# Modulation vectors on ScalarE and GpSimd, a scan for the summed decays, shorter Newton steps

## The chip, the core and the metric

The kernel runs on one core of a Trainium2 chip. The metric is the device time of one execution in microseconds (us), lower is better. TensorE is written PE here, VectorE DVE, ScalarE ACT, GpSimd POOL and SyncE SP, as the profile names them; PEld is PE's weight load.

## What is computed

Two transformer blocks run one after the other on 512 tokens of width 1024, in float32. What matters here is the first layer of the first block:

```python
mod = c_act @ ada_w[l] + ada_b[l]
sh1, sc1, g1, sh2, sc2, g2 = jnp.split(mod, 6, axis=-1)
hn = modulate(rms_norm(h, norm_mix_g[l]), sh1, sc1)
mix = hgrn2_mixer(hn, ...)       # chunks of 16 tokens, state carried along
h = h + g1 * mix
h = h + g2 * peer_ffn(modulate(rms_norm(h, norm_ffn_g[l]), sh2, sc2), ...)
```

and inside the mixer, for chunks of 16 tokens, `cum = jnp.cumsum(lfc, axis=2)`, the sum of the log decays within the chunk. Each `rms_norm` is `xf * lax.rsqrt(jnp.mean(xf * xf) + 1e-6)`. There are 14 modulation vectors of 1024 (six for each of two layers, two for the shared keys and values), each the product of one row of 1024 with a 1024 x 1024 matrix that is read once.

## The kernel before, in words

The 512 tokens are four tiles of 128. The first stage (0 to about 290 us) computes most of the 14 modulation vectors and, beside them, the mixer for tiles 0 and 1. Then the expert lookup `peer` (4 tiles, twice) gathers 64 rows of 8 KB for each token; beside it run the mixer for tiles 2 and 3, the attention of the second layer and the start of the second block. The last stage (from about 2250 us) is the mixture of experts of the second block.

`ada_vec` (line 243) makes one modulation vector, in two halves of 512 columns. Each half is a tile `aw` of 128 x 8 x 512 (2 MB), loaded in one transfer; four such buffers turn in a ring. Vectors 0 and 1 are loaded on SP's queue, the later ones on POOL's queue, where nothing else stands in this stage. A half is reduced over its 8 slices in one of two ways. With `pe` set, PE multiplies by the 128 x 32 tile `ca32` into PSUM (`ad<-aw,ca`, line 113; the program has 8 multiplications of 32 x 512 for a half, the trace shows 16), and ACT copies the sum to `aacc` (line 270). Without it DVE does one multiplication (line 272) and seven multiply-adds (line 275). Then PE adds `aacc` over the 128 rows, to columns (`ad<-kf,aacc`) or to a row (`ad<-aacc,kf`). The list `ADA` (line 1720) says which vector goes which way: 3, 12 and 7 on PE, five others on DVE. Vectors 8 and 9 (`ADA_MID`) and 10 and 11 (`ADA_LATE`) are on PE too.

`hgrn` (line 346) is the mixer, a sequence of steps that `Beside` interleaves with the vectors: normed rows are turned into `hTa` (`norm_T`, line 181), then there are eight heads; for each head PE makes the projections `pj`, ACT makes exponentials, tanh and logarithms, and DVE makes the products. Lines 414 to 420 are the sum of the log decays in chunks of 16: four rounds, each with one DVE addition (line 417) and one ACT copy of the part that has no partner (line 419), in turn between `lfa` and `lfb`.

`rsqrt` (line 161) is a Newton iteration on DVE for one or two columns: three operations to start (lines 164 to 166), then three rounds of three (lines 168 to 170). It is called in every norm.

Within an engine instructions run in the order in which a scheduler put them when the kernel was built; by that order an instruction that waits holds all that stand behind it on its engine. The rings of buffers decide when a transfer can start.

Of the kernel before, what the change touches and what calls it, by code (L numbers as in the profile page):

```python
# [11 lines left out]
F32 = mybir.dt.float32  # L12
I32 = mybir.dt.int32
U32 = mybir.dt.uint32
AF = mybir.ActivationFunctionType
ALU = mybir.AluOpType
# [4 lines left out]
P = 128  # L21
# [4 lines left out]
EPS = 1e-6  # L26
# [64 lines left out]
class K:  # L91
# [69 lines left out]
    def rsqrt(self, x, n, scale):  # L161
        nc = self.nc
        m, t, r = (self.sp.tile([P, n], F32, tag=f"{w}{n}", name=f"{w}{n}") for w in ("rsm", "rst", "rsr"))
        nc.vector.tensor_scalar(m, x, scale, EPS, op0=ALU.mult, op1=ALU.add)
        nc.vector.tensor_scalar(t.bitcast(I32), m.bitcast(I32), 1, None, op0=ALU.logical_shift_right)
        nc.vector.tensor_scalar(r.bitcast(I32), t.bitcast(I32), -1.0, float(0x5F3759DF), op0=ALU.mult, op1=ALU.add)
        for _ in range(3):
            nc.vector.tensor_tensor(out=t, in0=m, in1=r, op=ALU.mult)
            nc.vector.scalar_tensor_tensor(t, t, -0.5, r, op0=ALU.mult, op1=ALU.mult)
            nc.vector.scalar_tensor_tensor(r, t, 1.5, r, op0=ALU.add, op1=ALU.mult)  # L170
        return r

# [67 lines left out]

    def ada_vec(self, j, col, pe, tag="ad"):
        nc = self.nc
        pool = self.ap
        if col:
            pc = self.psum(tag)
            dst = self.cp.tile([P, 8], F32, name=f"ac{j}")
        else:
            dst = self.dp.tile([1, D], F32, name=f"ar{j}")  # L250
        for half in range(2):
            ch = 2 * j + half
            src = self.a["adaw"][ch]
            if self.aring:
                w = self.aring.tile([P, 8, 512], F32, tag="aw", name="aw")
                (nc.sync if j < 2 else nc.gpsimd).dma_start(w, src)
                w = [w[:, k, :] for k in range(8)]
            else:
                w = []
                for k in (0, 4):  # L260
                    g = self.gp.tile([P, 2 * D], F32, tag="g", name="g").rearrange("p (k n) -> p k n", k=4)
                    nc.sync.dma_start(g, src[:, k : k + 4, :])
                    w += [g[:, i, :] for i in range(4)]
            acc = pool.tile([P, 512], F32, tag="aacc", name="aacc", bufs=2)
            if pe:
                ps = self.psum(tag)
                for k in range(8):
                    g = 32 * (k % 4)
                    self.mm(ps[g : g + 32, :], self.ca32[:, k, :], w[k], start=k < 4, stop=k >= 4, tile_position=(0, g))
                nc.scalar.copy(acc, ps)  # L270
            else:
                nc.vector.tensor_scalar(acc, w[0], self.ca[:, 0:1], None, op0=ALU.mult)
                for k in range(1, 8):
                    nx = pool.tile([P, 512], F32, tag="aacc", name="aacc", bufs=2)
                    nc.vector.scalar_tensor_tensor(nx, w[k], self.ca[:, k : k + 1], acc, op0=ALU.mult, op1=ALU.add)
                    acc = nx
            if col:
                for q in range(4):
                    i = 4 * half + q
                    self.mm(pc[:, i : i + 1], acc[:, q * P : (q + 1) * P], self.ones[:, 0:1])  # L280
            else:
                rw = pool.tile([1, 512], F32, tag="arw", name="arw", bufs=3)
                nc.sync.dma_start(rw, self.a["adab"][ch : ch + 1, :])
                pr = self.psum(tag)
                self.mm(pr[0:1, :], self.ones[:, 0:1], acc)
                nc.vector.tensor_tensor(out=rw, in0=rw, in1=pr[0:1, :], op=ALU.add)
                nc.scalar.dma_start(dst[:, half * 512 : half * 512 + 512], rw)
        if col:
            n = 76 + 8 * COL.index(j)
            nc.vector.tensor_tensor(out=dst, in0=pc[:, 0:8], in1=self.cv[:, n : n + 8], op=ALU.add)  # L290
            self.col[j] = dst
        else:
            self.row[j] = dst
# [52 lines left out]
    def hgrn(self, tiles, gs, sh, bufs, whole=False):  # L346
        nc = self.nc
        es = ExitStack()
        nt = len(tiles)
        T = nt * P  # L350
        pa = self.pool("hgA", es=es)

        def ew(shape, tag, b=bufs):
            return pa.tile([P] + shape, F32, tag=tag, name=tag, bufs=b)

        def zeroed(name):
            z = pa.tile([P, T], F32, name=name)
            nc.vector.memset(z, 0.0)
            return z

        scb = [zeroed(f"scb{j}") for j in range(2)]
        kx = {n: zeroed(f"kx{n}") for n in (16, 32, 64)}
        qx = {n: zeroed(f"qx{n}") for n in (32, 64)}
        half = lambda x, n, j: x.rearrange("p (c j t) -> p c j t", j=2, t=n)[:, :, j, :]
        ch = lambda x, n: x.rearrange("p (c t) -> p c t", t=n)
        hTa = pa.tile([P, KC, T], F32, name="hTa")
# [6 lines left out]
        for hd in range(8):  # L373
            q2 = hd % 2
            if q2 == 0:
                w = self.weights(self.a["hgw"][4 * (hd // 2) + 3])
# [7 lines left out]
            w = self.weights(self.a["hgw"][4 * (hd // 2) + q2])  # L384
# [25 lines left out]
            lf = ew([T], "lfa")  # L410
            nc.scalar.activation(lf, e, AF.Ln, scale=self.lb[:, hc], bias=1.0)
            nc.scalar.activation(e, e, AF.Ln, bias=1.0)
            nc.vector.tensor_tensor(out=lf, in0=lf, in1=e, op=ALU.subtract)
            cum = lf
            for n, d in enumerate((1, 2, 4, 8)):
                nx = ew([T], "lfb", 1) if n % 2 == 0 else ew([T], "lfa")
                nc.vector.tensor_tensor(out=ch(nx, 16)[:, :, d:], in0=ch(cum, 16)[:, :, d:],
                                        in1=ch(cum, 16)[:, :, : 16 - d], op=ALU.add)
                nc.scalar.copy(ch(nx, 16)[:, :, :d], ch(cum, 16)[:, :, :d])
                cum = nx  # L420
            yield

            qs = ew([T], "qs")
# [7 lines left out]
            for n in (16, 32, 64):  # L431
                x = half(kx[n], n, 0)
                nc.vector.tensor_tensor(out=x, in0=half(cum, n, 0)[:, :, n - 1 : n].broadcast_to([P, T // (2 * n), n]),
                                        in1=half(cum, n, 0), op=ALU.subtract)
# [4 lines left out]
                else:  # L439
# [5 lines left out]
                                        in1=half(cum, n, 0)[:, :, n - 1 : n].broadcast_to([P, T // (2 * n), n]), op=ALU.add)  # L445
# [3 lines left out]
                                    in1=ch(cum, P), op=ALU.subtract)  # L449
# [36 lines left out]
            for i in range(nt):  # L486
                sl = slice(i * P, (i + 1) * P)
                nc.scalar.activation(o2[:, sl], po[:, sl], AF.Square, accum_out=ss[:, i : i + 1])
            r = self.rsqrt(ss, nt, 0.25 / P)
            on = ew([T], "ks")  # L490
            nc.vector.tensor_tensor(
                out=ch(on, P), in0=ch(po[:, :T], P), in1=r.unsqueeze(2).broadcast_to([P, nt, P]), op=ALU.mult)
# [19 lines left out]
        if whole:  # L512
            w = [self.weights(self.a["hgwo"][c]) for c in range(4)]
# [4 lines left out]
        else:  # L518
            for c in range(4):
                w = self.weights(self.a["hgwo"][c])  # L520
# [1067 lines left out]
    def run(self):  # L1588
# [23 lines left out]
        bg.advance(5 / 36)  # L1612
        for n, (j, pe) in enumerate(ADA):
            if n == 3:
# [102 lines left out]
        self.es.close()  # L1717


ADA = ((3, 1), (4, 0), (2, 0), (12, 1), (13, 0), (6, 0), (7, 1), (5, 0))  # L1720
ADA_LATE = ((10, 1), (11, 1))
COL = (0, 1, 6, 7, 12, 13)
ADA_MID = ((8, 1), (9, 1))
# [97 lines left out]
```

## Time and profile before

| | |
|---|---|
| median of 3 runs | 2770.45 us (2767.01 to 2771.69) |
| the profiled execution | 2769.54 us |
| its span, first to last instruction | 2767.7 us |
| TensorE's mean granted clock | 0.930 |
| PE, PEld busy | 85%, 54% of the span |
| DVE, ACT, POOL busy | 69%, 29%, 28% |
| HBM traffic over the span | 355 GB/s |

The span is 1.84 us shorter than the execution that it was recorded in. The profile has the busy time of each engine, a list of instruction groups by line with what they waited for, a timeline, and a chain of waits: the work that ended last, followed back from the last instruction, at each step to what released it.

### The profile page before, as it was taken

What the parts mean: (1) busy time and instruction counts of PE and PEld (TensorE: products, weight loads), DVE (VectorE), ACT (ScalarE), POOL (GpSimd) and SP (SyncE); (2) the same over time, 40 slices, a digit from 0 to 9 for tenths busy, and PEclk for the clock granted to TensorE, in tenths of its full rate; (3) what the DMA queues carried; (4) which work ended last, traced back from release to release, by engine and by line L of the source; (5) the groups of instructions that cost most, each with busy time, mean ns of one, the idle gap of its engine ahead of it and who ended that gap; (6) DMA issues with size and microseconds to landing.
All of it is one profiled execution on the core that took longest, in us unless ns stands there. A gap on an engine that the chain in (4) does not pass through costs nothing.

```text
span 2767.7 us, 30061 instructions
## 1 busy us (share of the span) xinstructions
PE 2340.0 (85%) x9714; PEld 1481.2 (54%) x9714; DVE 1918.3 (69%) x5370; ACT 795.0 (29%) x1891; POOL 777.0 (28%) x607
## 2 busy tenths in 40 slices
PE   5999888877988888579988858779999999988886
PEld 3786556644556555146656525437688754433322
DVE  3876898998996689984578799978787551111114
ACT  2543245562222632121383112142311310000001
POOL 0000123334333344443344334544440001111110
PEclk9999999998999889789999869889999999999999
DMA  9875889999989899999989889987999868999996
GB/s 413 325 281 189 321 311 357 380 378 375 374 356 406 330 350 384 336 369 401 370 307 371 326 312 341 363 327 289 390 413 363 298 237 364 424 426 425 423 425 280
DMA packets 124607, 976.22 MB, mean 353 GB/s; under 512 B 16830, under 2 KB 18238, under 8 KB 23584
## 3 DMA queue, kind: packets, MB, share of 16 engines
q0 software_dynamic: 82384, 591.04, 54.8%
q1 hardware_dynamic: 39280, 375.51, 33.4%
q10 hardware_dynamic: 2784, 7.73, 0.8%
q8 instruction: 79, 1.29, 0.2%
q14 instruction: 80, 0.66, 0.1%
HBM read 963.84 MB, written 19.43 MB: 355 GB/s over the span
## 4 chain that ended last, share of the span: by engine, by line
PE 43%; DVE 28%; DMA 16%; issue 6%; ACT 6%; POOL 1%; ACTq 0%; SPq 0%; POOLq 0%; DVEq 0%
PE pj L113 16%; DVE g L697 8%; DMA we<-in_we_dram 7%; DMA g<-in_uv_dram,ex 7%; PE acc L113 6%; PE gu L113 6%; PE mm L113 4%; DVE acc L716 4%; PE rt L113 3%; PE y L113 3%; DVE y L947 3%; PE ad L113 2%; POOL g L694 1%; DMA w<-in_hgw_dram 1%; PE mm L123 1%
## 5 line engine op out<-in xcount | busy, mean ns | idle before, releaser
L694 POOL DMA_INDIRECT g<-in_uv_dram,ex x512 | 695.3, 1358 | 1157.9 <-DVE acc L716 439.6
L113 PE MATMUL acc<-g,dg 128*128 128x512 f32 x1056 | 588.3, 690 | 191.4 <-ACT dg L708 191.0
L697 DVE SCALAR_TENSOR_TENSOR g<-g,hn 128x1024 f32<-128x1024 f32 x512 | 621.7, 1218 | 102.2 <-DMA g<-in_uv_dram,ex 100.0
L113 PEld LDWEIGHTS acc<-g,dg 128*128 128x128 f32 x1056 | 213.4, 215 | 440.2 <-ACT dg L708 261.3
L716 DVE SCALAR_TENSOR_TENSOR acc<-g,wt,acc 128x1024 f32<-128x1024 f32 x240 | 306.9, 1279 | 3.5
L113 PE MATMUL gu<-we,xT 128*64 128x512 f32 x1120 | 258.9, 601 | 19.3 <-DMA we<-in_we_dram 18.5
L113 PE MATMUL pj<-hT,w 128*128 128x256 f32 (+1 forms) x1136 | 216.2, 345 | 4.6 <-DMA w<-in_win_dram 3.1
L113 PEld LDWEIGHTS pj<-hT,w 128*128 128x128 f32 x1136 | 186.0, 193 | 39.6 <-issue 16.8
L113 PEld LDWEIGHTS gu<-we,xT 128*64 128x64 f32 x1120 | 100.5, 138 | 166.3 <-issue 115.2
L113 PE MATMUL pj<-hTa,w 128*128 128x256 f32 x768 | 181.1, 381 | 0.9 <-DVE sg L408 0.9
L113 PE MATMUL pj<-w,hT 128*128 128x256 f32 (+1 forms) x832 | 179.1, 373 | 0.0
L1433 DVE SCALAR_TENSOR_TENSOR th<-th,gu 128x256 f32<-128x256 f32 x35 | 14.7, 421 | 233.3 <-ACT th L1432 233.3
L701 ACT ACTIVATE wt<-hid 128x2 f32<-128x2 f32 x256 | 51.8, 203 | 422.8 <-DVE g L697 421.5
L113 PEld LDWEIGHTS pj<-w,hT 128*128 128x128 f32 x832 | 153.7, 192 | 27.4 <-issue 8.4
L1398 POOL DMA_INDIRECT xg<-xd,gi x31 | 32.0, 1033 | 449.3 <-PE tr L123 233.1
L113 PEld LDWEIGHTS pj<-hTa,w 128*128 128x128 f32 x768 | 141.2, 191 | 24.2 <-issue 5.6
L113 PE MATMUL y<-we,hT 128*64 128x512 f32 x560 | 143.3, 597 | 3.4 <-ACT hT L1442 0.4
L113 PE MATMUL rt<-hn2T,w 128*128 128x256 f32 (+1 forms) x640 | 124.7, 343 | 1.6 <-ACT hn2T L585 1.6
L708 ACT ACTIVATE dg<-kf,wt 128x128 f32<-128x128 f32 x264 | 101.5, 397 | 80.4 <-DVE wt L702 72.0
L947 DVE SCALAR_TENSOR_TENSOR y<-vb,wdw,y 128x128 f32<-128x128 f32 (+1 forms) x360 | 121.1, 387 | 1.4 <-ACT y L943 0.6
L1432 ACT ACTIVATE th<-gu 128x256 f32<-128x256 f32 x35 | 13.4, 383 | 368.8 <-PE gu L113 368.8
L113 PEld LDWEIGHTS rt<-hn2T,w 128*128 128x128 f32 x640 | 103.1, 194 | 22.9 <-issue 11.5
(482 smaller groups left out, 3309.3 us busy)
## 6 DMA issues: line engine op xcount, KB each, us to landing
we<-in_we_dram SPq DMA_DIRECT2D x96, 2048.0 KB
aw<-in_adaw_dram POOLq DMA_DIRECT2D x20, 2048.0 KB, 9.5
w<-in_win_dram SPq DMA_DIRECT2D x34, 1024.0 KB
w<-in_hgw_dram SPq DMA_DIRECT2D x32, 1024.0 KB
w<-in_pwq_dram SPq DMA_DIRECT2D x16, 1024.0 KB
w<-in_kvw_dram SPq DMA_DIRECT2D x16, 1024.0 KB
aw<-in_adaw_dram SPq DMA_DIRECT2D x4, 2048.0 KB
w<-in_hgwo_dram SPq DMA_DIRECT2D x8, 1024.0 KB
```

The costliest lines, as they stand in the source:

```text
L113: return self.nc.tensor.matmul(out, lhsT, rhs, start=start, stop=stop, **kw)
L123: return self.nc.tensor.transpose(out, in_, self.ident[:n, :n])
L694: nc.gpsimd.indirect_dma_start(out=g, out_offset=None, in_=uv, in_offset=bass.IndirectOffsetOnAxis(ap=picks[r // 16][0][:, r % 16 : r % 16 ...
L697: nc.vector.scalar_tensor_tensor(g[:, 0:D], g[:, 0:D], 1.0, hn, op0=ALU.mult, op1=ALU.mult, accum_out=hid[:, r : r + 1])
L701: nc.scalar.activation(wt[:, bs], hid[:, bs], AF.Gelu)
L708: nc.scalar.activation(dg, self.ident, AF.Copy, scale=wr)
L716: nc.vector.scalar_tensor_tensor(acc, g[:, D:], wr, acc, op0=ALU.mult, op1=ALU.add)
L947: nc.vector.scalar_tensor_tensor(y[:, c, :], vb[:, c, j : j + T], self.wdw[:, c, j : j + 1], y[:, c, :], op0=ALU.mult, op1=ALU.add)
L1398: self.nc.gpsimd.indirect_dma_start(out=xg, out_offset=None, in_=self.xd.rearrange("s (h d) -> (s h) d", h=2), in_offset=bass.IndirectOffs ...
L1432: nc.scalar.activation(th, pg[:, :256], AF.Tanh, scale=0.5)
L1433: nc.vector.scalar_tensor_tensor(th, th, 1.0, pg[:, :256], op0=ALU.add, op1=ALU.mult)
```

## The change

Three things change. Vectors 3, 12 and 7 get the mark 2 in `ADA`: ACT multiplies the eight slices of a half in place in `aw`, with the column of `ca` as a scale, and POOL adds the eight slices with seven additions into `aacc`. PE's final addition over the rows stays. The sum of the log decays becomes one DVE instruction, a scan of state = on16 * state + lf, where `on16` is a new constant tile that is 0 at each chunk's first token and 1 elsewhere. In `rsqrt` the factor -0.5 is put into the start value, so that a Newton round for one column has two operations in the place of three; for two columns it keeps three.

```diff
@@ rsqrt
-        nc.vector.tensor_scalar(m, x, scale, EPS, op0=ALU.mult, op1=ALU.add)
+        nc.vector.tensor_scalar(m, x, -0.5 * scale, -0.5 * EPS, op0=ALU.mult, op1=ALU.add)
         nc.vector.tensor_scalar(t.bitcast(I32), m.bitcast(I32), 1, None, op0=ALU.logical_shift_right)
-        nc.vector.tensor_scalar(r.bitcast(I32), t.bitcast(I32), -1.0, float(0x5F3759DF), op0=ALU.mult, op1=ALU.add)
+        nc.vector.tensor_scalar(r.bitcast(I32), t.bitcast(I32), -1.0, float(0x5F3759DF + 0x40000000 - 0x400000),
+                                op0=ALU.mult, op1=ALU.add)
         for _ in range(3):
-            nc.vector.tensor_tensor(out=t, in0=m, in1=r, op=ALU.mult)
-            nc.vector.scalar_tensor_tensor(t, t, -0.5, r, op0=ALU.mult, op1=ALU.mult)
+            if n == 1:
+                nc.vector.scalar_tensor_tensor(t, r, m, r, op0=ALU.mult, op1=ALU.mult)
+            else:
+                nc.vector.tensor_tensor(out=t, in0=m, in1=r, op=ALU.mult)
+                nc.vector.tensor_tensor(out=t, in0=t, in1=r, op=ALU.mult)
             nc.vector.scalar_tensor_tensor(r, t, 1.5, r, op0=ALU.add, op1=ALU.mult)
@@ ada_vec
-            if pe:
+            if pe == 2:
+                for k in range(8):
+                    nc.scalar.activation(w[k], w[k], AF.Copy, scale=self.ca[:, k : k + 1])
+                for k in range(1, 8):
+                    nc.gpsimd.tensor_tensor(out=acc, in0=w[0] if k == 1 else acc, in1=w[k], op=ALU.add)
+            elif pe:
@@ hgrn
+        on16 = pa.tile([P, T], F32, name="on16")
+        nc.vector.memset(on16, 1.0)
+        nc.vector.memset(on16.rearrange("p (c t) -> p c t", t=16)[:, :, 0:1], 0.0)
...
-            cum = lf
-            for n, d in enumerate((1, 2, 4, 8)):
-                nx = ew([T], "lfb", 1) if n % 2 == 0 else ew([T], "lfa")
-                nc.vector.tensor_tensor(out=ch(nx, 16)[:, :, d:], in0=ch(cum, 16)[:, :, d:],
-                                        in1=ch(cum, 16)[:, :, : 16 - d], op=ALU.add)
-                nc.scalar.copy(ch(nx, 16)[:, :, :d], ch(cum, 16)[:, :, :d])
-                cum = nx
+            cum = ew([T], "lfa")
+            nc.vector.tensor_tensor_scan(cum, on16, lf, 0.0, ALU.mult, ALU.add)
@@ the list of vectors
-ADA = ((3, 1), (4, 0), (2, 0), (12, 1), (13, 0), (6, 0), (7, 1), (5, 0))
+ADA = ((3, 2), (4, 0), (2, 0), (12, 2), (13, 0), (6, 0), (7, 2), (5, 0))
```

The scheduler puts the engines' instructions in a new order. Three places matter here. First POOL, from its start to the gathers of `peer` and what follows them, before (`aw` is the tile of a half, `g` a gathered row, line 256 the load):

```order
L231 MEMSET ca_106 128x256
L256 DMA aw<-in_adaw_dram 128x4096 x20
L694 DMA g<-in_uv_dram,ex 128x2048 x512
L211 MEMSET g 128x2048
L213 DMA picked<-g 128x2048 x4
```

and in the change, from the first load to the second half of vector 12 (the load is line 262 there, the additions line 275):

```order
L262 DMA aw<-in_adaw_dram 128x4096 x2
L275 ISA
L275 TENSOR_TENSOR aacc<-aw 128x512 x2
L275 TENSOR_TENSOR aacc<-aacc,aw 128x512 x12
L262 DMA aw<-in_adaw_dram 128x4096 x7
L275 TENSOR_TENSOR aacc<-aw 128x512
L262 DMA aw<-in_adaw_dram 128x4096
L275 TENSOR_TENSOR aacc<-aacc,aw 128x512
L275 TENSOR_TENSOR aacc<-aw 128x512
L275 TENSOR_TENSOR aacc<-aacc,aw 128x512 x10
L262 DMA aw<-in_adaw_dram 128x4096
L275 TENSOR_TENSOR aacc<-aacc,aw 128x512
```

The loads of vector 4 (the third and fourth on this queue) now stand behind all 14 additions of vector 3, and 13 of the 14 additions of vector 12 stand behind the load of the second half of vector 13. Second ACT in the first norm, where it takes the sum of vector 0 out of PSUM (`aacc<-ad`) and makes the first columns of `hTa`, before:

```order
L184 ACTIVATE xr<-h_63,rsr_233 128x1024
L270 COPY aacc<-ad 128x512 x2
L191 ACTIVATE hTa<-mm,ac_171,gs_208 128x128 x4
L184 ACTIVATE xr<-h_64,rsr_270 128x1024
L382 COPY v<-pj 128x256
```

and in the change:

```order
L189 ACTIVATE xr<-h_63,rsr_236 128x1024
L281 COPY aacc<-ad 128x512
L273 ACTIVATE aw<-aw,ca 128x512 x7
L281 COPY aacc<-ad 128x512
L273 ACTIVATE aw<-aw,ca 128x512
L196 ACTIVATE hTa<-mm,ac_171,gs_208 128x128
L273 ACTIVATE aw<-aw,ca 128x512
L196 ACTIVATE hTa<-mm,ac_171,gs_208 128x128
```

Seven multiplications of vector 3 stand between the two copies of vector 0, and others between the columns of `hTa`. Third PE after the state update of the third head, before:

```order
L113 MATMUL mm<-st,q 128x128
L113 MATMUL ad<-aw,ca_106 32x512 x7
L113 MATMUL pj<-w,hTa 128x256 x5
L113 MATMUL ad<-kf,aacc 128x1 x4
L113 MATMUL ad<-aw,ca_106 32x512 x8
L113 MATMUL pj<-w,hTa 128x256
L123 MATMUL mm<-kf,ks 128x128 x2
```

and in the change:

```order
L113 MATMUL mm<-st,q 128x128
L113 MATMUL pj<-w,hTa 128x256 x11
L113 MATMUL ad<-kf,aacc 128x1 x4
L113 MATMUL pj<-w,hTa 128x256
L123 MATMUL mm<-kf,ks 128x128 x2
```

The multiplications of vector 12 are gone from PE, and its addition over the rows (`ad<-kf,aacc`), which now waits for POOL, stands at about the same place among the projections.

## Rows read from the trace of the kernel before

**Rows 1.** The page's chain of waits, shares of the span by engine.

```profile
PE 43%; DVE 28%; DMA 16%; issue 6%; ACT 6%; POOL 1%; ACTq 0%; SPq 0%; POOLq 0%; DVEq 0%
```

**Rows 2.** Windows: stretch and length, busy us of each engine, PE clock, DMA, GB/s.

```profile
25.00:50.00 25.00, 18.66 (x89) 8.57 (x89) 4.22 (x24) 5.55 (x9) 1.05 (x2) 0.93 1.01 429
...
75.00:100.00 25.00, 25.00 (x129) 20.16 (x128) 24.78 (x72) 11.09 (x31) 1.22 (x2) 1.00 0.83 311
75.00:200.00 125.00, 124.29 (x679) 99.01 (x681) 105.56 (x328) 64.89 (x169) 5.97 (x11) 1.00 0.79 297
```

**Rows 3.** Timeline of PE: start, us, engine, line, operation, count, wait before it.

```profile
38.19 1.04 PE L113 MATMUL ad<-aw,ca 128*32 128x512 f32 x2
41.84 0.70 PE L113 MATMUL pj<-w,hTa 128*128 128x256 f32 x2 [2.34 <-DMA w<-in_hgw_dram]
43.60 1.92 PE L113 MATMUL ad<-aw,ca 128*32 128x512 f32 x4
...
65.21 1.06 PE L113 MATMUL ad<-aw,ca 128*32 128x512 f32 x6
...
129.91 1.93 PE L113 MATMUL ad<-aw,ca 128*32 128x512 f32 x16
```

**Rows 4.** Lines of ACT: count, ns least/median/most, first and last start, shapes.

```profile
L184 ACT ACTIVATE xr<-h,rsr x4: 1136/1148/1149, 27.3 to 351.1; 128x1024 f32<-128x1024 f32 x4
L708 ACT ACTIVATE dg<-kf,wt x264: 384/401/413, 313.3 to 2035.4; 128x128 f32<-128x128 f32 x132
L411 ACT ACT_TABLE_LOAD  x16: 1283/1283/1283, 62.8 to 601.2; - x16
```

**Rows 5.** Timeline of ACT and POOL, and loads of `aw` started at 16.93 and 24.36.

```profile
32.79 0.58 ACT L270 COPY aacc<-ad 128x512 f32<-128x512 f32 x1 [4.38 <-PE ad L113]
36.57 0.58 ACT L270 COPY aacc<-ad 128x512 f32<-128x512 f32 x1 [3.19 <-PE ad L113]
...
33.05 0.53 POOL L256 DMA_DIRECT2D aw<-in_adaw_dram  x1 [8.11 <-PE ad L113]
...
DMA to landing us min/median/max: 15.1/15.1/15.1
...
DMA to landing us min/median/max: 15.6/15.6/15.6
```

**Rows 6.** Lines of DVE and POOL for the price of an addition of 128 x 512.

```profile
L275 DVE SCALAR_TENSOR_TENSOR aacc<-aw,ca,aacc x84: 729/745/753, 11.1 to 222.7; 128x512 f32<-128x512 f32 x84
L211 POOL MEMSET g<- x1: 1806/1806/1806, 2080.7 to 2080.7; 128x2048 f32 x1
```

**Rows 7.** A line of DVE, and one of its runs beside POOL, from two timelines.

```profile
L645 DVE TENSOR_SCALAR fi<-flat x32: 156/169/422, 279.1 to 1688.8; 128x16 int32<-128x16 int32 x32
...
1597.24 0.93 POOL L694 DMA_INDIRECT g<-in_uv_dram,ex  x1 [0.30 <-issue]
...
1597.75 0.42 DVE L645 TENSOR_SCALAR fi<-flat 128x16 int32<-128x16 int32 x1
```

**Rows 8.** Lines of DVE in the sum of the log decays.

```profile
L413 DVE TENSOR_TENSOR lfa<-lfa,e x16: 410/418/426, 65.1 to 608.5; 128x256 f32<-128x256 f32 x16
L417 DVE TENSOR_TENSOR lfb<-lfa x32: 338/374/409, 65.6 to 612.4; 128x240 f32<-128x240 f32 x16, 128x192 f32<-128x192 f32 x16
L417 DVE TENSOR_TENSOR lfa<-lfb x32: 273/332/393, 66.1 to 615.1; 128x224 f32<-128x224 f32 x16, 128x128 f32<-128x128 f32 x16
```

**Rows 9.** The page's busy times of DVE and ACT, and a line of the Newton step.

```profile
PE 2340.0 (85%) x9714; PEld 1481.2 (54%) x9714; DVE 1918.3 (69%) x5370; ACT 795.0 (29%) x1891; POOL 777.0 (28%) x607
...
L168 DVE TENSOR_TENSOR rst<-rsm,rsr x165: 136/155/185, 23.2 to 2760.5; 128x1 f32<-128x1 f32 x114, 128x2 f32<-128x2 f32 x51
```

**Rows 10.** A line of POOL: the gathers of `peer`.

```profile
L694 POOL DMA_INDIRECT g<-in_uv_dram,ex x512: 932/1054/11518, 292.6 to 2076.6; - x171
```

## The prediction

> **What bounds the kernel now.** I read the chain of waits first, then the windows, then the timelines of the first stage. The chain says that PE holds 43% of the span and DVE 28%, with DMA at 16% and POOL at 1% [rows 1]. So a microsecond off PE or DVE can count, and POOL has time to give. The windows say where [rows 2]: from 75 to 200 us PE is busy 124.3 of 125 us, at the full clock, while DVE is busy 105.6 (24.78 of the first 25), ACT 64.9 and POOL 6.0. In this stage PE is the bound and DVE stands close behind it. From 25 to 50 us PE is busy 18.7 of 25 and the DMA share is full: there PE waits for the first weights of the mixer, which land at 41.84 after 2.34 us of idle time [rows 3].
>
> **PE's multiplications, removed.** Six halves with 16 matmuls each leave PE, 96 in all. Sixteen take 1.93 us at 129.91 [rows 3], 0.12 us each. Ten of the first half's sixteen run before 52 us, in the gaps of a PE that waits for other things (38.19, 43.60), and are worth nothing; the last six of that half run at 65.21, when PE is already packed. So 86 count: 86 x 0.12 = **10.4 us off the path**, as long as PE stays the bound.
>
> **ACT's multiplications, added.** The nearest rows also scale an SBUF tile by a column: 0.40 us for 128 x 128 and 1.15 us for 128 x 1024 [rows 4]. A line between them gives 0.72 us for 512 columns, 34.6 us for 48; six copies of 0.58 leave. ACT was busy 64.9 of 125 us from 75 to 200 [rows 2], so the sum is covered. One place is not clearly covered: seven of them now stand ahead of the second copy of vector 0, on which every column of hTa hangs. Their data land at 16.93 + 15.1 = 32.0 us, the first copy ends at 33.4 [rows 5], seven take 5.0 us, and the second copy runs at 38.4 and not at 36.57. The 1.9 us are hidden as long as the weights land only at 41.84 [rows 3]; if these come earlier, 1.9 us is the price. I take 0.
>
> **POOL's additions, added.** The trace has no addition on POOL. From below the price is DVE's 0.745 us for the multiply-add of 128 x 512; from above it is three passes (two reads, one write) at the rate of POOL's own memset of 128 x 2048, 1.806 us, so 3 x 0.45 = 1.35 us [rows 6]. I take the middle, 1.05 us, since the row below is the same shape on another engine and the row above is the same engine doing something else: 42 x 1.05 = 44 us, on an engine with almost nothing else to do there. The Trainium skill (GPSIMD Engine Reference, Performance versus the Vector engine) gives 4.50 us for 2048 columns, which by columns is an estimate of 1.12 us; with it the term on DVE below would grow by 28 x 0.07 x 0.84 = 1.6 us.
>
> Two things stand behind these additions. First, POOL's own loads. The load of vector 4 was issued at 33.05 us [rows 5]; now it waits for all 14 additions of vector 3. That vector's second half lands at 24.36 + 15.6 = 40.0 us [rows 5], and ACT then needs until some 53 us for the 16 multiplications (11.5 us) and the hTa columns between them; the additions end at about 55, and a load takes 9 to 16 us more. DVE asks for it right after the first head's scan, at some 66 us (the sum before it starts at 65.1 [rows 8]). That is 0 to 5 us late, and I take **+1 us**; in return the mixer's weights share the full DMA queues of 25 to 75 us with two loads fewer, for which I take nothing.
>
> Second, DVE. One row shows that POOL's work can stretch an instruction of DVE: a tensor-scalar of 16 columns takes 0.42 us when POOL is preparing a gather at the same moment, and 0.169 us as a rule [rows 7]. If an addition held DVE's two-operand work for its whole length, the 28 additions of vectors 12 and 7 would take 29.4 us from it, times its busy share of 105.6/125 [rows 2] = 24.8 us. The scans give six heads 3.6 us back there (next part). DVE's own idle time in the stretch is 19.4 us; I take three quarters of it as lying where it is needed, 14.6. That leaves **+6.6 us** that PE waits. The bounds are 0 (no hold) and 21 us (a full hold and no idle time of use).
>
> **The scan.** For each of 16 heads four additions, 2 x 0.374 + 2 x 0.332 = 1.41 us, and four copies on ACT go; one scan comes [rows 8]. No row has a scan. One pass over 128 x 256 takes 0.42 us, the four additions together 1.41; I take 0.80, nearer the single pass, because an element needs two chained operations and is still visited once. So 0.6 us a head. In the first stage it went into the term above. In the second mixer call, beside the gathers, 8 x 0.6 = 4.9 us of DVE's time go. There DVE lies on the chain for 28% of the span, 775 us of its 1918 busy [rows 1, 9], 0.40 us of path for each busy microsecond: **-2.0 us**. In the new order ACT has 174 table loads in the program and not 163, and all eleven more stand in this second call, where the exponentials and logarithms meet the gathers' Gelu: 11 x 1.283 = 14.1 us [rows 4], at ACT's 6% of the span for 795 us busy [rows 1, 9], 0.21: **+3.0 us**.
>
> **The Newton step.** The trace has 114 runs of line 168 with one column, three for each of 38 calls, at 0.155 us [rows 9]; the 17 calls with two columns keep their count. Four of the calls fall into the first stage, where PE is the bound; the other 34 save 34 x 3 x 0.155 = 15.8 us of DVE's time, times 0.40: **-6.3 us**. The new operations are of the same size as those that they replace, so nothing is added. The memsets of on16 run at the very start, beside the first load, and once more in the second call, and I count them at nothing.
>
> **The sum.** -10.4 + 1 + 6.6 - 2.0 + 3.0 - 6.3 = -8.1 us against the profiled execution of 2769.5 us, so 2761.4. The median of the runs is 0.9 us above that execution, and I forecast **2762 us**. The last stage moves along with the rest, since its loads start when the stages before it free their buffers.
>
> **The rivals.** *DVE becomes the bound of the first stage.* The additions hold DVE fully, and its idle time lies elsewhere. With half of its idle time of use, 24.8 - 3.6 - 9.7 = 11.5 us stand where I put 6.6, 5 more; additions at 1.35 us add 28 x 0.3 x 0.84 = 7 more; and longer additions make the load of vector 4 some 3 us later still. That is 2762 + 15 = **2777 us**, slower than before. It decides from the point at which 13 additions behind the load of vector 13 take longer than the third head's work on PE ahead of the waiting matmul, some 15 us; at 1.05 us and one DVE operation between two additions that point is reached. For it speaks DVE at 24.78 of 25 us [rows 2]; against it that PE stayed packed in that very window. The Trainium skill states the mechanism as a rule: by SBUF — State Buffer, Who interferes with whom, a DVE instruction with two SBUF inputs contends with a POOL instruction that reads SBUF, and the second to start is blocked until the first is through. By that rule this rival is the forecast; the trace agrees in sign (0.42 against 0.169 us) and has no addition to show the size.
>
> *Full cover.* The additions hold nobody, for 0 in the place of 6.6: **2755 us**. For it speaks that ACT's multiplications space the additions out; against it the stretched row [rows 7].
>
> *Nothing.* The 10.4 us of the first stage go into its own waits, and of the 8.3 us of DVE's time later only half count, since DVE then comes earlier to gathers that have not landed (DMA is 16% of the chain [rows 1]): +1 + 3.0 - 4.2 leaves nothing, **2770 us**.
>
> *It does less than it says.* Newton steps for two columns keep three operations, so one call in three gains nothing; that is in the sum.
>
> **How the numbers follow.** Forecast 0.35, DVE as the bound 0.25, full cover 0.22, nothing 0.18. The forecast's own range is 2756 to 2768: its late load between 0 and 5, the scan between 0.42 and 1.41 us (-4 to 0), the share of DVE's time on the path between 0.2 and 0.6. With the other cases the range that holds eight in ten is 2750 to 2778. A measurement of this kernel tells about 0.2%, 5.5 us, from no change: faster means under 2764.9, slower above 2776. Faster: 0.25 of the forecast's 0.35, full cover 0.22, a little of the rest, 0.50. Slower: half of the first rival and little else, 0.16. The rest is 0.34.
>
> **What the profile would show.** If the first step is right, PE's busy time falls by some 11 us and the eighth head's work ends earlier by what I left of it. If DVE is held, DVE's products of the mixer run longer than 0.42 us beside POOL's additions, and PE's matmuls over the rows wait for POOL. The scan's row gives its price. The DVE time of the Newton lines should fall by 18 us. I am wrong if the stage up to the first gather at 292.6 us [rows 10], which should come some 3 us earlier, comes later; or if it comes over 10 us earlier, so that nothing was held.

## The result, and the profile after

The change makes the kernel slower: 2790.7 us against 2771.7 (medians of five runs each); the ratio of the runs is 1.0064 with a 95% interval of 1.0048 to 1.0080. That is outside the range, on the other side of the forecast. The profiled execution took 2800.55 us, 10 above its median. In the two profiled executions the loss has one place: the first gather comes at 323.5 us and not at 292.6 [rows 10], and from there to the end of the span both kernels need the same, 2475.3 and 2475.1 us. The medians differ by 19 us and the first gathers by 30.9. So if the first stage is as long in every execution, which isn't shown (each kernel was traced once), some 12 us come back behind the first gather in a median execution of the change; the scan alone gains some 4 us there.

The page of the changed kernel, busy time and chain of waits, to be read against [rows 9] and [rows 1]:

```profile
PE 2334.2 (83%) x9618; PEld 1486.7 (53%) x9618; DVE 1936.8 (69%) x5212; ACT 822.3 (29%) x1880; POOL 823.5 (29%) x649
PE 35%; DVE 31%; DMA 17%; issue 8%; ACT 6%; POOL 2%; ACTq 0%; POOLq 0%; DVEq 0%; SPq 0%
```

PE's busy time fell by 5.8 us, but DVE's rose by 18.5 though 158 of its instructions are gone, and PE's share of the chain fell from 43% to 35%. Its windows (columns as in [rows 2]) show where:

```profile
125.00:150.00 25.00, 10.28 (x44) 8.84 (x44) 21.07 (x20) 6.96 (x14) 18.14 (x17) 0.66 0.62 240
143.00:149.00 6.00, 5.74 (x21) 5.23 (x22) 2.25 (x8) 4.58 (x10) 0.47 (x1) 0.50 0.96 408
200.00:225.00 25.00, 8.49 (x45) 7.43 (x44) 23.07 (x21) 2.53 (x9) 18.94 (x17) 0.66 0.54 204
75.00:200.00 125.00, 105.95 (x540) 87.64 (x538) 106.86 (x268) 70.74 (x155) 22.72 (x23) 0.92 0.72 279
```

From 75 to 200 us PE is busy 106.0 us where it was 124.3 [rows 2]. In the two windows of 25 us DVE is busy 21 and 23 us with only 20 and 21 instructions, while POOL is busy 18 and 19 us. The timeline of the changed kernel there (DVE, POOL and PE, columns as in [rows 3]; other rows are left out between these):

```profile
125.56 0.56 POOL L262 DMA_DIRECT2D aw<-in_adaw_dram  x1
126.95 14.01 DVE L421 TENSOR_SCALAR e<-e 128x256 f32<-128x256 f32 x1
128.59 12.22 POOL L275 TENSOR_TENSOR aacc<-aacc,aw 128x512 f32<-128x512 f32 x10
140.76 0.56 POOL L262 DMA_DIRECT2D aw<-in_adaw_dram  x1
143.26 0.66 PE L123 MATMUL mm<-kf,e 128*128 128x128 f32 x2 [14.58 <-DVE e L461]
143.72 1.06 PE L113 MATMUL pj<-hTa,w 128*128 128x256 f32 x2
...
203.36 0.56 POOL L262 DMA_DIRECT2D aw<-in_adaw_dram  x1
203.59 15.16 DVE L443 TENSOR_TENSOR kx<-lfa 128x128 f32<-128x128 f32 x1
206.38 12.22 POOL L275 TENSOR_TENSOR aacc<-aacc,aw 128x512 f32<-128x512 f32 x10
221.02 1.22 PE L113 MATMUL mm<-qx,kx 128*128 128x128 f32 x4 [16.51 <-DVE kx L446]
```

One tensor-scalar of 256 columns, 0.29 us elsewhere, lasts 14.01 us, and one product of 128 columns, 0.28 us elsewhere, 15.16: each is held until POOL's unbroken train of additions is over and POOL issues its next load. Everything behind it waits, and PE stands for 14.6 and 16.5 us. When PE goes on, two matmuls take 1.06 us where the same two take 0.60 at 203.91: after standing still PE has a granted clock of 0.50 from 143 to 149 us, the lower of its two levels, and is busy 5.74 of these 6 us. From 221 to 224 us it is the same. By the two times, 1.06 for 0.60, the lower clock costs an estimated 4 us behind the two waits.

The lines of the new operations and of the gathers, and PE's waits from 45 to 325 us (us in total, times, longest):

```profile
L275 POOL TENSOR_TENSOR aacc<-aacc,aw x36: 1249/1254/1295, 46.3 to 219.1; 128x512 f32<-128x512 f32 x36
L273 ACT ACTIVATE aw<-aw,ca x48: 706/710/725, 32.7 to 199.3; 128x512 f32<-128x512 f32 x48
L430 DVE TENSOR_TENSOR_SCAN lfa<-on,lfa x16: 676/684/693, 65.3 to 627.4; 128x256 f32<-128x256 f32 x16
L171 DVE SCALAR_TENSOR_TENSOR rst<-rsr,rsm x114: 196/215/221, 23.1 to 2791.1; 128x1 f32<-128x1 f32 x114
L704 POOL DMA_INDIRECT g<-in_uv_dram,ex x512: 932/1103/10721, 323.5 to 2110.6; - x171
```

```profile
PE mm L113 <- DVE kx L446: 16.5, 1, 16.5
PE mm L123 <- DVE e L461: 16.4, 3, 14.6
PE mm L113 <- DVE ks L438: 5.6, 3, 3.6
```

The third wait holds the late load of vector 4: POOL issues it at 60.97 us, DVE waits for the data until 70.37, PE for DVE until 71.91.

```profile
60.97 2.14 POOL L262 DMA_DIRECT2D aw<-in_adaw_dram  x4
70.37 0.48 DVE L283 TENSOR_SCALAR aacc<-aw,ca 128x512 f32<-128x512 f32 x1 [3.50 <-DMA aw<-in_adaw_dram]
71.91 1.22 PE L113 MATMUL mm<-qs,ks 128*128 128x128 f32 x4 [3.62 <-DVE ks L438]
```

### The profile page after: what moved, and what is told of

The parts are those of the page before. It is cut to its first block, busy times and chain, and to the rows that moved or that the text cites. A ratio compares the mean times of both kernels' runs of the same rounds, so it can differ in the third digit from the quotient of the medians.

```text
span 2798.8 us, 29692 instructions
## 1 busy us (share of the span) xinstructions
PE 2334.2 (83%) x9618; PEld 1486.7 (53%) x9618; DVE 1936.8 (69%) x5212; ACT 822.3 (29%) x1880; POOL 823.5 (29%) x649
## 4 chain that ended last, share of the span: by engine, by line
PE 35%; DVE 31%; DMA 17%; issue 8%; ACT 6%; POOL 2%; ACTq 0%; POOLq 0%; DVEq 0%; SPq 0%
PE pj L113 12%; DVE g L707 9%; DMA g<-in_uv_dram,ex 7%; DMA we<-in_we_dram 7%; PE acc L113 6%; PE gu L113 5%; DVE y L957 4%; DVE acc L726 4%; PE y L113 3%; PE mm L113 3%; PE rt L113 3%; DMA aw<-in_adaw_dram 2%; POOL g L704 1%; PE mm L123 1%; PE ad L113 1%
## 5 line engine op out<-in xcount | busy, mean ns | idle before, releaser
L113 PE MATMUL acc<-g,dg 128*128 128x512 f32 x1056 | 595.7, 699 | 186.5 <-ACT dg L718 185.9
```

Source lines behind the costliest of these rows:

```text
L113: return self.nc.tensor.matmul(out, lhsT, rhs, start=start, stop=stop, **kw)
```

## The experiments

All times are against the kernel before on the same chip. "First gather" is read from the one trace of each run and stands for the length of the first stage.

| run | ratio to before, 95% interval | first gather, us | longest DVE operation, 45 to 250 us |
|---|---|---|---|
| the kernel before | 1 | 292.6 | under 1 |
| the change | 1.0064 [1.0048, 1.0080] | 323.5 | 15.16 |
| scan and Newton step only | 0.9954 [0.9937, 0.9972] | 288.4 | under 1 |
| the same, vector 3 on POOL | 0.9950 [0.9937, 0.9963] | 287.2 | under 1 |
| additions spaced by ACT | 1.0094 [1.0069, 1.0120] | 321.4 | 1.34 |
| vectors only | 1.0072 [1.0057, 1.0086] | 317.5 | 15.06 |
| Newton step only | 1.0010 [0.9993, 1.0027] | 292.4 | under 1 |
| scan only | 0.9967 [0.9952, 0.9982] | 287.7 | under 1 |
| vector 3 on POOL, vector 4 loaded by SP | 0.9938 [0.9921, 0.9954] | 284.2 | under 1 |
| memsets for the additions | 0.9926 [0.9909, 0.9943] | 281.6 | 1.52 |
| later loads on SP | 1.0029 [1.0016, 1.0042] | 296.4 | 1.49 |
| vector 3 on POOL, vector 4 loaded by SP, Newton step as before | 0.9933 [0.9920, 0.9945] | 284.8 | under 1 |
| vector 12 on POOL | 0.9998 [0.9982, 1.0013] | 300.6 | 14.42 |
| gaps between the additions | 1.0038 [1.0020, 1.0057] | 316.9 | 3.81 |
| vector 12, no load in its train | 0.9991 [0.9976, 1.0006] | 296.3 | 1.49 |
| vector 12, a load of 2 KB in it | 0.9982 [0.9965, 0.9998] | 296.3 | 12.12 |

### Which part loses

```diff
@@ scan and Newton step only: of the change
-ADA = ((3, 2), (4, 0), (2, 0), (12, 2), (13, 0), (6, 0), (7, 2), (5, 0))
+ADA = ((3, 1), (4, 0), (2, 0), (12, 1), (13, 0), (6, 0), (7, 1), (5, 0))
@@ vectors only: of the kernel before
+            if pe == 2:
+                for k in range(8):
+                    nc.scalar.activation(w[k], w[k], AF.Copy, scale=self.ca[:, k : k + 1])
+                for k in range(1, 8):
+                    nc.gpsimd.tensor_tensor(out=acc, in0=w[0] if k == 1 else acc, in1=w[k], op=ALU.add)
-            if pe:
+            elif pe:
...
-ADA = ((3, 1), (4, 0), (2, 0), (12, 1), (13, 0), (6, 0), (7, 1), (5, 0))
+ADA = ((3, 2), (4, 0), (2, 0), (12, 2), (13, 0), (6, 0), (7, 2), (5, 0))
```

> The changed kernel with vectors 3, 12 and 7 back on PE, so that only the scan and the Newton steps are left of the change. Theory A (two unbroken trains of additions on POOL, each of which holds DVE for its whole length of 14 to 15 us, and the late load of vector 4 are the loss): both waits of 14.6 and 16.5 us on PE are gone, the first gather comes at 288 to 292 us, and the time is 2762 to 2767 us, 4 to 9 below the kernel before. Theory B (a part of the loss comes from the scan, the eleven more table loads or the new order of the mixer): 2772 us or more, and the first gather later than 293 us.

> The kernel before with only the three vectors moved to ACT and POOL; sum of the decays and Newton step as before. Theory A: the loss of the changed kernel without the gain of its other two parts: first gather at 318 to 330 us, time 2793 to 2802 us. Theory B: less slow than the changed kernel, 2770 to 2785 us.

Without the vectors the kernel is 0.46% faster than before and the two waits are gone; with the vectors alone it is 0.72% slower. The gain of the other two parts was there, and the vectors took it and more. So theory A holds in where the loss lies, but not in all of its mechanism. With the vectors alone only vector 12's train holds one DVE operation, for 15.06 us. Beside vector 7's train, as unbroken, no operation is held longer than 1.48 us, and PE waits at most 4.2 us there:

```profile
198.87 15.65 POOL L269 TENSOR_TENSOR aacc<-aacc,aw 128x512 f32<-128x512 f32 x12
208.23 1.34 DVE L441 TENSOR_TENSOR kx<-kx,kk 128x128 f32<-128x128 f32 x1
```

What makes one train hold DVE to its end and lets the other take turns with it is taken up under "One hold for the whole train, or turns?".

### Does the place of the train matter, or the gap between additions?

```diff
@@ vector 3 on POOL (vector 12 on POOL has the 2 at 12 alone)
+ADA = ((3, 2), (4, 0), (2, 0), (12, 1), (13, 0), (6, 0), (7, 1), (5, 0))
@@ additions spaced by ACT
-                for k in range(8):
-                    nc.scalar.activation(w[k], w[k], AF.Copy, scale=self.ca[:, k : k + 1])
+                nc.scalar.activation(acc, w[0], AF.Copy, scale=self.ca[:, 0:1])
                 for k in range(1, 8):
+                    at = pool.tile([P, 512], F32, tag="at", name="at", bufs=1)
-                    nc.gpsimd.tensor_tensor(out=acc, in0=w[0] if k == 1 else acc, in1=w[k], op=ALU.add)
+                    nc.scalar.activation(at, w[k], AF.Copy, scale=self.ca[:, k : k + 1])
+                    nc.gpsimd.tensor_tensor(out=acc, in0=acc, in1=at, op=ALU.add)
```

> The changed kernel with only vector 3 on ACT and POOL, vectors 12 and 7 back on PE. Its 14 additions run at 46 to 61 us, while DVE has only work that reads PSUM, or none. Theory A: no DVE instruction is held for more than 1.5 us, but the loads of vector 4 still stand behind the additions (issued at 61 us, not at 33), so PE waits 3 to 6 us; time 2766 to 2772 us, 3 to 6 above the kernel without POOL's additions. Theory C (any train of additions costs its length, wherever it stands): 14 us above that kernel, 2777 or more.

> The changed kernel with vector 12 alone on ACT and POOL, vectors 3 and 7 back on PE: the counterpart of the run with vector 3 alone, the same 14 additions at another place. Theory A (what a train costs is set by DVE's work beside it): one DVE operation of 12 to 15 us at about 125 us, one wait of some 14 us on PE, first gather 10 to 14 us later than in the run with vector 3 alone (287.2), at 297 to 301 us; time 8 to 14 us above that run. Theory B (one train is harmless, only two add up): within 3 us of that run.

> The changed kernel with the same 42 additions on POOL, but ACT writes each multiplied slice into one small tile of its own, so that the next addition can only start after ACT's next multiplication (0.71 us and the signals), and POOL sits idle between two additions. Theory A (DVE gets in as soon as POOL has a gap; what cost so much is the train without a gap): no DVE instruction longer than 1.8 us in the stage, no PE wait over 4 us, the first gather at 295 to 305 us, time 2768 to 2780 us. Theory D (each addition takes 1.25 us from DVE wherever it stands, 28 x 1.25 = 35 us less DVE's idle time): as the changed kernel or slower, 2788 to 2800 us.

The place decides most of it. Vector 3's 14 additions (46 to 61 us) cost nothing that shows, 0.9950 against 0.9954, where theory A had 3 to 6 us for the late load; the same 14 additions of vector 12 move the first gather from 287.2 to 300.6 us and the ratio from 0.9950 to 0.9998. (The two trains also differ in the loads that POOL issues between the additions; without such a load vector 12's first gather is still at 296.3 us, see "One hold for the whole train, or turns?".) In the trace of vector 12 alone the train meets one tensor-scalar of DVE:

```profile
123.16 14.42 DVE L424 TENSOR_SCALAR kk<-kk,nho,ho 128x256 f32<-128x256 f32 x1
```

The spaced run was half a miss. No DVE operation lasts over 1.34 us, as theory A has it, but the time, 1.0094, is worse than the change's. Most of the spaced additions lie at 66 to 98, 135 to 179 and 211 to 255 us, where DVE is needed, vector 3's among them. From 62 us to the first gather 29 operations of DVE are held by more than 0.3 us there, for 24 us in all against their usual lengths; in the change six are, for 33 us. Shorter holds alone save nothing.

### What holds DVE

```diff
@@ memsets for the additions (aw is the tile of w)
-                    nc.gpsimd.tensor_tensor(out=acc, in0=w[0] if k == 1 else acc, in1=w[k], op=ALU.add)
+                    nc.gpsimd.memset(aw[:, 0:1400] if k < 7 else acc, 0.0)
@@ gaps between the additions
                     nc.gpsimd.tensor_tensor(out=acc, in0=w[0] if k == 1 else acc, in1=w[k], op=ALU.add)
+                    if k < 7:
+                        nc.gpsimd.memset(w[k][:, 0:256], 0.0)
@@ later loads on SP
-                (nc.sync if j < 2 else nc.gpsimd).dma_start(w, src)
+                (nc.gpsimd if j == 3 else nc.sync).dma_start(w, src)
```

> The changed kernel with every addition on POOL replaced by a memset (of 128 x 1400 of the slices' tile, and once a half of aacc, to 0), which writes as long but reads nothing; vectors 3, 12 and 7 are left out of the computation. Theory A (what holds DVE is that both engines read SBUF at once): no two-input operation of DVE is held for longer than 1.5 us, PE has no wait of over 4 us in the stage, and the first gather comes at 285 to 292 us, the time 15 us or more below the changed kernel. Theory B (any work of POOL on SBUF holds DVE): single operations of DVE of 8 to 15 us remain, and the time is that of the changed kernel, 2787 to 2797 us.

> The changed kernel with a memset of 128 x 256 (0.31 us, into a slice that has been added) on POOL between two additions of a half. Theory A (the hold ends at the first moment in which POOL does not read): no DVE operation is longer than 1.8 us, DVE gets one or two operations into each gap; the stalls of PE are shorter, but DVE still loses about a microsecond for each addition, so the time is 2780 to 2795 us. Theory F (POOL keeps the hold until it has nothing more to do): DVE operations of 12 us and more remain, and the time is 2790 us or more.

> The changed kernel with the loads of all vectors after vector 3 on SP's queue, so that no addition on POOL stands behind a load. Theory A (an unbroken train of additions holds DVE, whatever made the train): ACT delivers a slice in 0.71 us and POOL needs 1.25, so trains still form; single DVE operations of 5 to 15 us remain and the time is 2780 to 2792 us. Theory P (the waiting load makes the pile, and without it the additions are spread): no DVE operation over 4 us, first gather before 300 us, time 2760 to 2775 us.

The memsets of 128 x 1400, 1.27 us each, are as long as the additions, and the first gather comes at 281.6 us, 42 earlier than in the change. The timeline of DVE and POOL in that run:

```profile
154.81 5.42 POOL L276 MEMSET aw<- 128x1400 f32 x4
...
155.33 0.28 DVE L455 TENSOR_TENSOR lfa<-lfa 128x128 f32<-128x128 f32 x1
155.53 0.85 DVE L284 TENSOR_SCALAR aacc<-aw,ca 128x512 f32<-128x512 f32 x1
156.30 0.27 DVE L444 TENSOR_TENSOR kx<-lfa 128x128 f32<-128x128 f32 x1
...
183.60 1.52 DVE L422 TENSOR_SCALAR e<-e 128x256 f32<-128x256 f32 x1
183.68 2.64 POOL L276 MEMSET aw<- 128x1400 f32 x2
```

Operations with two SBUF inputs run beside a writing POOL at their usual 0.28 us; tensor-scalars with one input are still held, for 1.52 us at most. So two-input work is held by POOL's reads and not by its writes. ACT does its 48 multiplications in this run too, so ACT's work isn't the price either. The 42 us are not all the price of the reads, though: the memset of `aacc` needs no slice, so PE's addition over the rows does not wait for a whole train here, and the scheduler gave the memsets another order, in trains of at most four beside the mixer's heads.

With gaps the longest hold is of a tensor-scalar:

```profile
128.35 3.81 DVE L426 TENSOR_SCALAR kk<-kk,nho,ho 128x256 f32<-128x256 f32 x1
```

It is longer than theory A's 1.8 us, for it lasts through the first gap, a memset at 129.98 us, and ends beside the second, two memsets at 131.45. Gaps do cut the hold short; as expected under theory A the time stays above the kernel before. The run with the later loads on SP surprised: its trains of additions have no gap over 0.08 us, and yet no hold is over 1.49 us. DVE and POOL take turns, about one held DVE operation for each addition. Theory A had 5 to 15 us there. Theory P has the holds and the first gather right, for another reason than its own, and the time wrong: 2779.6 us, where it had at most 2775. PE's waits are now for POOL itself, since the addition over the rows stands in PE's order and the work behind it waits with it:

```profile
129.65 1.86 PE L113 MATMUL ad<-kf,aacc 128*128 128x1 f32 x8 [8.42 <-POOL aacc L275]
```

### One hold for the whole train, or turns?

In all trains that locked DVE out so far, two in the change and one each with the vectors alone and with vector 12 alone, POOL issues a load between the first additions and the rest; where they take turns, none. Two runs put that to the test on vector 12 alone.

```diff
@@ no load in its train: of vector 12 on POOL
-                (nc.sync if j < 2 else nc.gpsimd).dma_start(w, src)
+                (nc.sync if j < 2 or j == 13 else nc.gpsimd).dma_start(w, src)
@@ a load of 2 KB in it: of that
                     nc.gpsimd.tensor_tensor(out=acc, in0=w[0] if k == 1 else acc, in1=w[k], op=ALU.add)
+                    if half == 0 and k == 2:
+                        nc.gpsimd.dma_start(w[1][0:1, :], self.a["adab"][0:1, :])
```

> Vector 12 alone on ACT and POOL as before, but the loads of vector 13 are on SP's queue, so that no load is issued on POOL between vector 12's additions. Theory L (a load that POOL issues inside the train is what locks DVE out for the rest of it): no DVE operation is longer than 1.7 us, DVE and POOL take turns, PE's wait is 3 to 9 us instead of 14.4, first gather at 290 to 296 us instead of 300.6. Theory U (it is chance, or which DVE operation meets the train): one DVE operation of 10 to 15 us is still there, first gather at 298 to 302 us.

> The same, with one load of 2 KB issued on POOL's queue after the second addition of vector 12's first half, into a part of the slices' tile that has been added (no load of vector 13 there). Theory L: the lock-out is back: one DVE operation of 10 to 15 us, first gather at 298 to 302 us. Theory U: as the run without a load in the train, whatever that shows.

The timelines of the two runs, first without the load:

```profile
123.84 1.48 DVE L428 TENSOR_TENSOR lfa<-lfa,e 128x256 f32<-128x256 f32 x1
125.51 1.49 DVE L430 TENSOR_TENSOR_SCAN lfa<-on,lfa 128x256 f32<-128x256 f32 x1
127.04 1.17 DVE L443 TENSOR_TENSOR kx<-lfa 128x128 f32<-128x128 f32 x1
...
125.01 13.23 POOL L275 TENSOR_TENSOR aacc<-aacc,aw 128x512 f32<-128x512 f32 x10
...
137.07 1.87 PE L113 MATMUL ad<-kf,aacc 128*128 128x1 f32 x8 [10.26 <-POOL aacc L275]
```

and with it:

```profile
123.74 0.54 POOL L277 DMA_DIRECT2D aw<-in_adab_dram  x1
124.30 1.28 POOL L275 TENSOR_TENSOR aacc<-aacc,aw 128x512 f32<-128x512 f32 x1
126.75 9.78 POOL L275 TENSOR_TENSOR aacc<-aacc,aw 128x512 f32<-128x512 f32 x8
136.48 0.58 POOL L262 DMA_DIRECT2D aw<-in_adaw_dram  x1
...
124.96 12.12 DVE L432 TENSOR_TENSOR_SCAN lfa<-on,lfa 128x256 f32<-128x256 f32 x1
...
135.36 1.87 PE L113 MATMUL ad<-kf,aacc 128*128 128x1 f32 x8 [8.53 <-POOL aacc L275]
```

Theory L holds in what it says of DVE: 2 KB of load bring the lock-out back (12.12 us on a scan that takes 0.69). It ends at POOL's next load, where the train stops as well; which of the two frees DVE the runs don't separate. (In the first run POOL's next load, at 138.19, stands before the last addition.) The run without the load also shows the price of turns: POOL needs 13.23 us for ten additions and not 12.2. In the time theory L missed. The first gather is the same in both, 296.3 us, because PE waits for the end of POOL's train anyway, 10.26 and 8.53 us at the addition over the rows, where theory L had 3 to 9. Against vector 12 alone as it was (300.6) 4 us are gained, but not by the turns, since the run with the lock-out gains them too; both have vector 13's loads on SP. In total time the three don't differ beyond their intervals.

### The scan, the Newton step, and a version that beats both

> The kernel before with only the two-operation Newton step. The first operation of a round takes 0.214 us in the traces of the changed kernel and of its part without POOL, not 0.155 as I had assumed, so a round saves 0.31 - 0.214 = 0.096 us and 34 calls after the first stage 9.8 us of DVE's time. Theory A (that time lies on the path for 0.4 of it): 4 us below the kernel before, first gather unchanged at 291 to 294 us. Theory B (it lies on the path nearly in full, since each operation of the chain waits for the one ahead): 8 to 11 us below. Theory C (nothing): within 2 us.

> The kernel before with only the scan for the sum of the log decays. Theory A: the first gather comes 4 us earlier as in the run with scan and Newton step, and the second mixer call gives 2 us less what the additional table loads take; 4 to 7 us below the kernel before. Theory B (the scan's gain is given back beside the gathers): within 2 us of the kernel before though the first gather is 4 us earlier. Theory C (the scan carries the whole gain of the two): 10 to 13 us below.

```diff
@@ vector 4 loaded by SP: of vector 3 on POOL; the last run also has rsqrt as before
-                (nc.sync if j < 2 else nc.gpsimd).dma_start(w, src)
+                (nc.sync if j < 2 or j == 4 else nc.gpsimd).dma_start(w, src)
```

> The kernel with the scan, the Newton step and vector 3 alone on ACT and POOL, but with the two loads of vector 4 on SP's queue, so that they don't stand behind vector 3's additions. Theory A (the load that stands behind the additions is what is left of the loss): the loads are issued at 33 to 45 us, PE's wait of 3.6 us at 72 us is gone, first gather at 283 to 286 us, time 2 to 5 us below the same kernel with those loads on POOL's queue. Theory B (the loads take the room that the mixer's weights have between 40 and 60 us): PE waits there instead, and the time is the same or up to 4 us more.

> The scan, vector 3 alone on ACT and POOL, the two loads of vector 4 on SP's queue, and the Newton step as before. Theory A (the Newton step is worth nothing): 0.991 to 0.996 of the kernel before, the same as with the shorter Newton step (0.9938). Theory B (the shorter step is worth some 4 us, which its run alone did not show): 0.995 to 0.998.

The Newton step alone gives nothing that can be measured (theory C), and taking it out of the best version costs nothing either. The scan alone gives 0.33%, 9 us, between theories A and C; the interval, 5 to 13 us, reaches into both. Why more than its busy time shows in one head of the second mixer call, before (DVE, then ACT):

```profile
444.22 0.41 DVE L413 TENSOR_TENSOR lfa<-lfa,e 128x256 f32<-128x256 f32 x1
445.87 0.39 DVE L417 TENSOR_TENSOR lfb<-lfa 128x240 f32<-128x240 f32 x1
452.46 0.29 DVE L417 TENSOR_TENSOR lfa<-lfb 128x128 f32<-128x128 f32 x1
...
450.01 0.30 ACT L419 COPY lfa<-lfb 128x128 f32<-128x128 f32 x1 [1.56 <-DVE wt L702]
454.12 0.42 ACT L424 ACTIVATE qs<-lfa 128x256 f32<-128x256 f32 x1
```

and a head with the scan (from the run of scan and Newton step):

```profile
437.30 0.41 DVE L428 TENSOR_TENSOR lfa<-lfa,e 128x256 f32<-128x256 f32 x1
437.97 0.68 DVE L430 TENSOR_TENSOR_SCAN lfa<-on,lfa 128x256 f32<-128x256 f32 x1
...
438.68 0.42 ACT L434 ACTIVATE qs<-lfa 128x256 f32<-128x256 f32 x1 [1.22 <-DVE lfa L430]
```

Four rounds that each cross from DVE to ACT stand in both engines' orders behind other work: from 444.63 to 454.12 us, 9.5 us for 1.39 us of additions (the last 1.3 us are a table load on ACT). With the scan it is 1.0 us. Over the eight heads beside the gathers the mean falls from 8.6 us to 2.2.

With vector 4's loads on SP's queue PE's wait of 3.1 us (3.6 in the change) for DVE's product is gone, and the first gather comes 3.0 us earlier than with vector 3 alone, as theory A has it; in the time the intervals overlap. That version beats both kernels, with the short Newton step (0.9938) or without (0.9933, 2754.3 against 2773.8 us).

## Why the prediction was wrong

- **PE's multiplications, 10.4 us.** The work was there to be saved: with the memsets PE is busy 244.4 us up to the first gather, against 256.8 in the run of scan and Newton step. Of that the first gather gains 6.8 us, with short holds of tensor-scalars still beside it. In the change PE's busy time over the span fell by 5.8 us and not by some 11; part of its work ran at the lower clock there.
- **ACT's multiplications.** 0.710 us measured, 0.72 taken. Vector 0's second copy ran at 39.09, near my 38.4, but by luck: ACT had been idle for 2.02 us and waited for PE, whose multiplications of that half began only when its data had landed, at 35.39.
- **POOL's additions.** 1.254 us, where I took 1.05 and had 1.35 as the bound. The load of vector 4 makes PE wait 3.6 us, where I took 1 from a range of 0 to 5.
- **DVE held by the additions, 6.6 us: this step failed.** I let an addition hold DVE for its own length, 29.4 us in all for 28, weighed by DVE's busy share, and let three quarters of DVE's idle time absorb them. The holds came to about that much, 14.01 and 15.16 us, but in two pieces: an instruction that is held while POOL's train goes on keeps DVE's whole order waiting, so the idle time lies outside the train and absorbs nothing. PE waited 14.6 and 16.5 us, 31.1 in all, against my bound of 21, and an estimated 4 us more went to the lower clock behind these waits, for which I had no term. All three terms of the vectors together were -10.4 + 1 + 6.6 = -2.8 us; between the runs without and with them the first gather moves by 35.1 us the other way. The row that I had, 0.42 against 0.169 us [rows 7], is of a one-input tensor-scalar beside the preparing of a gather: it is no case of two inputs against POOL's reads, and one short hold could not show the train.
- **The rival that DVE becomes the bound** named the mechanism, DVE held by POOL's reads, and came to 2777: the same sum with less idle time of use, so it too was short. The rule that I cited for it (the Trainium skill, SBUF — State Buffer, Who interferes with whom) speaks of a block by one instruction; the turns of 1.2 to 1.5 us agree with it, the 12 to 15 us after a load inside the train are more than it says. Two of these five long holds met tensor-scalars, which have one tile as input and which the rule as I cited it leaves out.
- **The scan, -2.0 us.** Sign right, size and mechanism wrong: 0.684 us an operation (0.80 taken), but I priced DVE's busy time and left out the elapsed time of four rounds over two engines. Alone it gives 9 us, 4.9 of them before the first gather, where I had counted it only as time given back to DVE. With the +3.0 us for table loads I had a loss of 1 us behind the first gather and some 4 us of gain came. The eleven additional loads are in the change's trace (174 against 163); what they cost isn't separated from that gain.
- **The Newton step, -6.3 us.** Nothing. Two fifths of it are a price that I had taken as unchanged: the new first operation, with a column as its scalar, takes 0.215 us, so a round saves 0.31 - 0.215 = 0.095 us, not 0.155, 9.7 us of DVE's time in 34 calls. Why nothing of the rest arrives isn't shown.

## What to carry to other kernels

Before work that reads SBUF goes to POOL, list what DVE does in those microseconds: the same 14 additions were free at 46 to 61 us, where DVE reads PSUM or waits, and moved the first gather by 13 us at 123. Keep POOL's own loads out of such a train: with the later loads on SP the first gather came 27 us earlier than in the change, of which the late load of vector 4 is some three. And remember that the consumer in PE's order waits for the train's end: for vector 12 alone that took as much time with turns as with one long hold. Price a chain that crosses engines by the time from its first input to its consumer, not by busy time.

## What the runs showed of the hardware

- Without a load inside, a train of additions on POOL and DVE's operations take turns (held operations last up to 1.5 us each); after POOL has issued a load inside the train, one DVE operation waits until the additions stop at POOL's next load, 12.1 to 15.2 us, five unbroken trains of five, a load of 2 KB being enough. Each kernel was traced once. What in the chip makes the difference wasn't tried.
- POOL's memsets hold DVE's one-input tensor-scalars (0.85 for 0.48, 1.52 for 0.28 us) and not its two-input operations.
- A scalar-tensor-tensor of one column takes 0.215 us with a column as its scalar; the operations it replaces take about 0.155.
